# Strassen's seven products in the output projection of a hybrid decoder step, with weight loads on ACT's queue

## The chip, the cores and the metric

The kernel runs on one core of a Trainium2 chip. The metric is the device time of one launch in microseconds (us). Three runs of the kernel before took 2503.86, 2506.80 and 2510.32 us, the median is 2506.8.

## What is computed

One decoder layer runs over a prompt of 1024 tokens (16 learned meta tokens ahead of it) and over 8 sample sequences of 8 tokens each. The input is normed and projected into queries, keys, values and gates; 16 heads of width 128 (6 mLSTM "A", 6 gated-delta "B", 4 HGRN "C") run their recurrences; their outputs are normed, gated and projected back. In the reference, cut to what matters here:

```python
h = _rmsnorm(x, norm_w)
proj = jnp.einsum('bld,de->ble', h, w_in)                 # d = 2048, e = 8984
...
hcat = jnp.concatenate([ha, hb, hc], axis=2)              # 16 heads x 128
hcat = hcat * lax.rsqrt(jnp.mean(hcat * hcat, axis=-1, keepdims=True) + EPS)
y = hcat.reshape(bsz, L, MIX) * out_norm_w * jax.nn.silu(z)
out = jnp.einsum('ble,ed->bld', y, w_out)                 # the output projection, 2048 x 2048
return x + out
...
y_prompt = _rmsnorm(xp[:, N_META:], final_norm_w)
y_sample = _rmsnorm(xs, final_norm_w)
```

All is float32. The kernel gets that accuracy on TensorE from the faster fp32r format by splitting each operand in a high and a low part: a product is hi x hi + hi x lo + lo x hi, three matmuls.

## The kernel before

**Halves.** The prompt is worked off in two halves of 512 tokens; the first takes the 64 sample and 16 meta tokens along. For each half the input projection runs over 17 groups of columns (one head's q, k, v and gates after the other, in the order of `ORDER`: C0 B0 A0 B1 A1 C1 B2 A2, then B3 A3 C2 B4 A4 B5 A5 C3). The recurrence of a head (`mlstm_scan`, `gdn_scan`, `hgrn_scan`), its finish (`finish`, line 836) and the preparation of the second half's input (`prep_B`) are generators. `Weave.pump` steps them between the projection's matmuls by a clock of estimated costs, in four queues ("scan", "fin", "post", "bg"), one generator of a queue at a time. The build then orders each engine's queue, so the order in the code is near to, but not always, the order on an engine.

**Weights.** A piece is 128 x 512 numbers of `w_in` or `w_out`, 256 KB. `w_raw` and `o_raw` load it into one of four raw buffers (`wraw`). `feed_split` lets ScalarE (ACT) cast it to `whi` and VectorE (DVE) subtract to `wlo`, four buffers each. `feed_ahead` splits up to three pieces ahead of TensorE (PE) and asks for the raw data four pieces further on. All loads and stores of the kernel are issued by SyncE (SP), in one queue and in order: a load of a raw buffer waits until DVE has read the old piece, and what stands behind it waits too. Each DMA also waits until the one eight DMAs earlier has landed; these waits show as DMAHW0 to DMAHW7 below.

**Finish.** `finish` norms a head's output, turns it through DRAM (`turn_out`, `turn_in`), multiplies by the gate, splits it (cast on ACT, subtraction on GpSimd, POOL) and writes both parts to `y_dram`.

**Output projection.** After the last column group, for each half and each unit of `OUT_UNITS` (a column group of 512 and its token tiles), 16 heads `k` are summed in PSUM banks `oacc`: three matmuls of 128x128 by 128x512 for each prompt tile, two for the sample tile, whose high and low parts share one matmul's rows. Then DVE adds the input `x`, ACT sums squares, POOL multiplies by the final norm's weight, and `final_norm` scales and stores. The second half's `y` is loaded during the last column group of the first half.

Of the kernel before, what the change touches and what calls it, by code (L numbers as in the profile page):

```python
# [6 lines left out]
F32 = mybir.dt.float32  # L7
# [6 lines left out]
P = 128  # L14
# [172 lines left out]
OUT_UNITS = ([(cg, range(5)) for cg in range(4)], [(cg, range(4)) for cg in range(3)] + [(3, range(2)), (3, range(2, 4))])  # L187
# [3 lines left out]
def hybrid_step(ctx, tc, i, o):  # L191
# [3 lines left out]
    DMA = nc.sync.dma_start  # L195
    weave = Weave(ck)
# [33 lines left out]
    def w_raw(col, g):  # L230
        raw = wp.tile([P, 512], F32, tag="wraw", name="wraw")
        v = raw.rearrange("p (k c) -> p k c", c=P)
        if col is None:
            V.memset(raw, 0.0)
            for src, at in ((C_AI, 0), (C_BB, 32), (C_AF, 64), (C_BA, 96)):
                DMA(v[:, :, at:at + HA], i["w_in"][0, 512 * g:512 * (g + 1), src:src + HA].rearrange("(k p) c -> p k c", p=P))
        else:
            DMA(v, i["w_in"][0, 512 * g:512 * (g + 1), col:col + P].rearrange("(k p) c -> p k c", p=P))
        return raw

    def o_raw(k, cg):
        raw = wp.tile([P, 512], F32, tag="wraw", name="wraw")
        DMA(raw, i["w_out"][0, P * k:P * (k + 1), 512 * cg:512 * (cg + 1)])
        return raw

# [95 lines left out]
    for units in OUT_UNITS:  # L341
        for cg, _ in units:
            for k in range(NK):
                pieces.append((o_raw, k, cg))
# [256 lines left out]
    y_dram = [dp.tile([NH, P, w], F32R, name=f"y{w}") for w in (2 * NSAMP + 2 * HALF, 2 * HALF)]  # L601
# [233 lines left out]

    def finish(half, head, outs, ssq, scale, zs):
        r = sp.tile([P, 16], F32, tag="hr", name="hr")
        for g in half.groups:
# [16 lines left out]
        turn_in(hrs[-1], d)  # L855
        ck.last = ck.t["T"] + 5.0
# [12 lines left out]
        S.copy(yhi[:, 0:W], y[:, 0:W])  # L869
        yield  # L870
        G.tensor_tensor(ylo[:, 0:W], y[:, 0:W], yhi[:, 0:W], op=ALU.subtract)
        yield
        d = y_dram[half.index][head].bitcast(F32)
        for part, t in enumerate((yhi, ylo)):
            t = t.bitcast(F32)
            at_ = 2 * NSAMP if half.first else 0
            DMA(d[:, at_ + HALF * part:at_ + HALF * (part + 1)], t[:, 0:HALF])
            if half.first:
                DMA(d[:, NSAMP * part:NSAMP * (part + 1)], t[:, HALF:WS])
# [90 lines left out]
    def mlstm_scan(half, h, kT, qT, vT, tho, zs, nm, em, st):  # L970
# [118 lines left out]
        weave.add("fin", finish(half, h, hxs, ssq, 0.25, zs))  # L1089
# [60 lines left out]
    def gdn_scan(half, h, ck_, cq, cv, zs, Gb, eG, bb, st):  # L1150
# [242 lines left out]
        weave.add("fin", finish(half, HA + h, hxs, ssq, 1.0, zs))  # L1393
# [22 lines left out]
    def hgrn_scan(half, h, kT, lf, qT, vT, zs, st):  # L1416
# [152 lines left out]
        weave.add("fin", finish(half, HA + HB + h, hxs, ssq, 0.25, zs))  # L1569
# [91 lines left out]
    def load_y(half, g):  # L1661
        w = y_dram[half.index].shape[-1]
        yT[half.index][g] = [hp.tile([P, 2, w], F32R, tag=f"h{g}{part}", name=f"y{g}{part}") for part in (0, 1)]
        for q in range(4):
            DMA(yT[half.index][g][q // 2][:, q % 2].bitcast(F32), y_dram[half.index][4 * g + q].bitcast(F32))

    def y_block(half, k, n, part):

        at_ = HALF * part + P * n
        return yT[half.index][k // 4][k % 4 // 2][:, k % 2, at_:at_ + P]  # L1670

    hB, yT = {}, [{}, {}]
    for half, groups in zip(halves, group_lists):
        if not half.first:
            weave.drain_queue("bg")
            hT = hB
        seen = set()
        for n, group in enumerate(groups):
# [8 lines left out]
            if n == len(groups) - 1:  # L1687
# [3 lines left out]
                else:  # L1691
                    after = lambda g: load_y(halves[0], g)
# [12 lines left out]

    ys_flat = o["y_sample"].rearrange("b t d -> (b t) d")
    tags = ["a", "b", "c", "d", "e", "f", "g", "h", "j", "a", "b", "c", "d", "e", "f", "g", "h", "j", "k", "u"]

    def final_norm(toks, some, res, ss, fr, late):
        for n in some:  # L1710
            cnt = toks[n][1]
            V.tensor_reduce(fr[:cnt, n:n + 1], ss[:cnt, n], op=ALU.add, axis=AX.X)
            V.tensor_scalar(fr[:cnt, 8 + n:9 + n], fr[:cnt, n:n + 1], 1.0 / D, EPS, op0=ALU.mult, op1=ALU.add)
            G.tensor_tensor(fr[:cnt, 16 + n:17 + n], fr[:cnt, 8 + n:9 + n], halfneg[:cnt, 0:1], op=ALU.pow)
        yield
        for n in some:
            _, cnt, _, dst = toks[n]
            for cg in range(4):
                t, r = res[n, cg], fr[:cnt, 16 + n:17 + n]
                if cg == 3 and late:  # L1720
                    V.scalar_tensor_tensor(t[:cnt], t[:cnt], r, fnw[cg][:cnt], op0=ALU.mult, op1=ALU.mult)
                elif cg == 3 or late and cg == 2:
# [4 lines left out]
                yield  # L1727

# [12 lines left out]
    fnw = []  # L1741
    for half in halves:
        toks = []
        for n, (c0, cnt) in enumerate(half.tiles):
            if half.first and n == 0:
                toks.append((0, NSAMP, xs_flat, ys_flat))
            else:
                a = HALF * half.index + c0
                toks.append((c0, P, i["x_prompt"][0, a:a + P], o["y_prompt"][0, a:a + P]))
        nt = len(toks)  # L1750
        ss = sp.tile([P, 8, 4], F32, tag="oss", name="oss")
        fr = sp.tile([P, 24], F32, tag="fr", name="fr")
        res = {}
        for cg, some in OUT_UNITS[half.index]:
            ccols = slice(512 * cg, 512 * (cg + 1))
# [78 lines left out]
```

## Time and profile before

| | before |
|---|---|
| median of three runs | 2506.8 us (2503.86 to 2510.32) |
| the profiled execution | 2506.0 us, span 2504.3 us |
| first and last start of an output projection matmul | 2102.3 and 2493.5 us |
| output projection matmuls (`oacc`) | 1088 with `whi`, 576 with `wlo` |
| mean granted TensorE clock | 0.99 |
| DMA: moved, mean rate | 350.82 MB, 140 GB/s |
| HBM read, written | 285.71 MB, 62.19 MB |

The span runs from the first instruction to the end of the last on any engine; the time of an execution has a little more around it. PE is matmul, PEld the load of the stationary operand, DVE VectorE, ACT ScalarE, POOL GpSimd, SPq SyncE's queue. In rows by group: line, engine, operation, out<-in, shapes, count | busy us, mean ns of one | idle time before them and what ended it. In rows of waits: who waited, for whom, us in total, times, the longest. Most instructions go through one wrapper and carry its line, 137, so tile names tell them apart.

### The profile page before, as it was taken

Reading aid. Unit: us, or ns where it says so; the run is one execution under the profiler, and the core shown is the slowest. Engines: PE = TensorE matmul, PEld = TensorE weight load, DVE = VectorE, ACT = ScalarE, POOL = GpSimd, SP = SyncE. Lnnn points to the kernel's source line nnn. Section 1 sums busy time; section 2 is a strip of 40 time slices with the busy share of each in tenths; the row PEclk is TensorE's granted clock in tenths of the full one; section 3 lists DMA queues with packets and bytes.
Section 4 is the critical chain, followed back from the end, with each engine's and each line's share of the span. In section 5 each row is a group of like instructions: output and inputs, shape, how many; then the busy total and the mean of one; then the engine's idle time right before and its main releaser. Section 6 shows DMA issues by size and latency. Waiting matters only on the chain.

```text
span 2504.3 us, 43941 instructions
## 1 busy us (share of the span) xinstructions
PE 2442.1 (98%) x16032; PEld 2184.5 (87%) x16032; DVE 1425.5 (57%) x3080; ACT 991.2 (40%) x2430; POOL 554.8 (22%) x743
## 2 busy tenths in 40 slices
PE   6999999999999999999999999999999999999998
PEld 5898999999999999999787888888888888888886
DVE  7775655765656655556864556554654545323435
ACT  5643434443435333333642434333443334222324
POOL 5331212420313312113320113110320102211201
PEclk9999999999999999999999999999999999999999
DMA  5656665655645454447554455454554558636735
GB/s 129 152 140 147 147 146 133 162 131 130 158 99 138 99 131 118 118 119 203 132 132 115 120 123 136 122 130 101 138 127 114 129 123 257 183 84 200 254 97 185
DMA packets 681045, 350.82 MB, mean 140 GB/s; under 512 B 260004, under 2 KB 622076, under 8 KB 680828
## 3 DMA queue, kind: packets, MB, share of 16 engines
q1 hardware_dynamic: 680828, 348.01, 54.3%
q8 instruction: 126, 2.06, 0.4%
q14 instruction: 91, 0.75, 0.1%
HBM read 285.71 MB, written 62.19 MB: 139 GB/s over the span
## 4 chain that ended last, share of the span: by engine, by line
PE 80%; issue 5%; DVE 5%; DMA 4%; ACT 2%; POOL 2%; SPq 1%; POOLq 0%; DVEq 0%; ACTq 0%
PE acc L137 59%; PE oacc L137 9%; PE pa L137 1%; DVE wlo L137 1%; PE po L137 1%; PE nd L137 1%; PE pz L137 1%; PE pyy L137 1%; DMA wraw<-in_w_in_dram 1%; POOL res L137 1%; PE pu L137 1%; DMA px<-in_x_prompt_dram 1%; ACT whi L137 1%; PE poh L137 1%; PE pw L137 1%
## 5 line engine op out<-in xcount | busy, mean ns | idle before, releaser
L137 DVE TENSOR_TENSOR wlo<-wraw,whi 128x512 fp32r<-128x512 f32 x720 | 525.6, 734 | 569.6 <-ACT whi L137 552.1
L137 PE MATMUL acc<-hA,whi 128*128 128x288 f32 (+1 forms) x4544 | 826.2, 304 | 11.3 <-ACT whi L137 6.4
L137 ACT CAST whi<-wraw 128x512 fp32r<-128x512 f32 x720 | 441.9, 618 | 929.1 <-PE acc L137 641.2
L137 PE MATMUL acc<-hB,whi 128*128 128x512 f32 x2272 | 722.2, 400 | 4.3 <-ACT whi L137 2.1
L137 PEld LDWEIGHTS acc<-hA,whi 128*128 128x128 f32 x4544 | 679.6, 191 | 18.2 <-ACT whi L137 8.1
L137 PE MATMUL acc<-hA,wlo 128*128 128x288 f32 x2240 | 489.7, 299 | 1.6 <-DVE wlo L137 1.6
L137 PEld LDWEIGHTS acc<-hB,whi 128*128 128x128 f32 x2272 | 413.6, 189 | 86.2 <-ACT whi L137 2.7
L137 PE MATMUL acc<-hB,wlo 128*128 128x512 f32 x1120 | 441.1, 394 | 2.6 <-DVE wlo L137 2.6
L137 PEld LDWEIGHTS acc<-hA,wlo 128*128 128x128 f32 x2240 | 367.7, 190 | 2.7 <-DVE wlo L137 2.6
L137 PE MATMUL oacc<-whi,y 128*128 128x512 f32 x1088 | 343.4, 390 | 1.1 <-ACT whi L137 1.1
L137 PEld LDWEIGHTS acc<-hB,wlo 128*128 128x128 f32 x1120 | 211.0, 188 | 52.0 <-DVE wlo L137 6.8
L137 PEld LDWEIGHTS oacc<-whi,y 128*128 128x128 f32 x1088 | 204.2, 188 | 44.5 <-ACT whi L137 2.4
L137 PE MATMUL oacc<-wlo,y 128*128 128x512 f32 x576 | 224.8, 390 | 1.2 <-DVE wlo L137 1.2
L137 PEld LDWEIGHTS oacc<-wlo,y 128*128 128x128 f32 x576 | 108.1, 188 | 25.2 <-DVE wlo L137 3.1
L137 POOL TENSOR_TENSOR res<-res,fnw 128x512 f32<-128x512 f32 (+1 forms) x34 | 54.3, 1627 | 255.4 <-ACT oscr L137 255.4
L137 POOL TENSOR_TENSOR y<-y,zs 128x592 fp32r<-128x592 f32 (+1 forms) x32 | 46.0, 1437 | 171.4 <-ACT zs L137 106.7
L137 POOL TENSOR_TENSOR qd<-qT,emb 128x512 f32<-128x512 f32 x12 | 17.7, 1479 | 230.3 <-PE po L137 230.3
L137 DVE TENSOR_TENSOR Yt<-Yc,Bb 128x60 f32<-128x60 f32 (+8 forms) x180 | 37.6, 209 | 43.9 <-DMA Bb<-db 39.0
L137 POOL TENSOR_TENSOR hr<-hr,halfneg 128x4 f32<-128x4 f32 (+1 forms) x48 | 44.1, 919 | 61.1 <-DVE hr L137 58.4
L137 POOL TENSOR_TENSOR nrm<-nrm,halfneg 128x10 f32<-128x10 f32 x12 | 23.5, 1960 | 138.9 <-DVE nrm L137 138.9
L137 POOL TENSOR_TENSOR X<-Ex,hk 128x256 f32<-128x256 f32 (+1 forms) x40 | 39.1, 978 | 63.2 <-PE pa L137 41.8
L137 ACT ACTIVATE Wt<-pw,nrm 128x128 f32<-128x128 f32 (+1 forms) x54 | 19.8, 367 | 78.1 <-PE pw L137 78.1
(416 smaller groups left out, 2766.7 us busy)
## 6 DMA issues: line engine op xcount, KB each, us to landing
wraw<-in_w_in_dram SPq DMA_DIRECT2D x564, 256.0 KB
wraw<-in_w_out_dram SPq DMA_DIRECT2D x144, 256.0 KB
y<-y SPq DMA_DIRECT2D x16, 576.0 KB
px<-in_x_prompt_dram SPq DMA_DIRECT2D x32, 256.0 KB
yd<-y SPq DMA_DIRECT2D x128, 64.0 KB
out_dram<-sst SPq DMA_DIRECT2D x16, 512.0 KB
s<-yd SPq DMA_DIRECT2D x32, 256.0 KB
y<-zs SPq DMA_DIRECT2D x32, 256.0 KB
```

What stands on the lines that cost most here:

```text
L137: return f(out, *a, **k)
```

## The change

**Strassen.** Write the prompt's product as a 2 x 2 block matrix: rows of tokens (first and second half), heads in `ORDER`'s first eight (K1) and last eight (K2), columns in two halves of 1024. Seven products of half size take the place of eight, by the Winograd form. The first and second use plain blocks of `y` and of `w_out`; the others use sums S1 to S4 of `y` blocks and T1 to T4 of `w_out` blocks. `phase(u, j, ...)` is one product's unit: 512 columns, four tiles, eight heads; `LAST_UNITS` cuts the last product's second unit in two. The samples' matmuls stand in the first three products (`own`, with the product's own weights, and `other`, with a weight piece of their own).

**The sums.** `combine_weights` makes T1 to T4 in the second half as a "bg" generator: 16 rounds of four loads, four POOL subtractions and four stores to DRAM. `finish` of the second half makes S1 to S4 and A22: the first half's plain `y` comes back from DRAM (`y_whole`), POOL adds and subtracts, and each result is split by a cast and a DVE subtraction and stored (`y_comb`). `load_y` with a name first drains the finishes that it needs. S2 is loaded in three steps during the second product, its last tile at the start of the third.

**Weights.** Pieces of full columns and all output pieces are issued by ACT (`WDMA`), into five raw buffers. The gate's small pieces stay on SP.

```diff
+K1, K2 = HEADS[:NH // 2], HEADS[NH // 2:]
+LAST_UNITS = [(0, range(4)), (1, range(2)), (1, range(2, 4))]
...
+    WDMA = nc.scalar.dma_start
...
-        raw = wp.tile([P, 512], F32, tag="wraw", name="wraw")
+        raw = wp.tile([P, 512], F32, tag="wraw", name="wraw", bufs=5)
...
-            DMA(v, i["w_in"][0, 512 * g:512 * (g + 1), col:col + P].rearrange("(k p) c -> p k c", p=P))
+            WDMA(v, i["w_in"][0, 512 * g:512 * (g + 1), col:col + P].rearrange("(k p) c -> p k c", p=P))
...
+    def c_raw(name, j, kk):
+        raw = wp.tile([P, 512], F32, tag="wraw", name="wraw", bufs=5)
+        WDMA(raw, w_comb[name][NK // 2 * j + kk])
+        return raw
...
     def finish(half, head, outs, ssq, scale, zs):
...
+        def parts(src, hi, name):
+            S.copy(hi, src)
+            ck.sync()
+            V.tensor_tensor(src.bitcast(F32R), src, hi, op=ALU.subtract)
+            d = y_comb[name][kk].bitcast(F32)
+            ck.last = max(ck.last, ck.t["T"]) + 3.0
+            yield
+            DMA(d[:, 0:HALF], hi.bitcast(F32))
+            DMA(d[:, HALF:], src)
+        if upper:
+            G.tensor_tensor(ya, ya, y, op=ALU.subtract)
...
+            yield from parts(ya, yhi, "S3")
+            return
+        G.tensor_tensor(yb, yb, y, op=ALU.add)
+        yield
+        yield from parts(y, yhi, "A22")
+        G.tensor_tensor(ya, yb, ya, op=ALU.subtract)
+        yield
+        yield from parts(yb, spare, "S1")
+        G.tensor_tensor(yc, yc, ya, op=ALU.subtract)
+        yield
+        yield from parts(ya, yhi, "S2")
+        yield
+        yield from parts(yc, spare, "S4")
...
+    def load_y(u, n, src):
+        if isinstance(src, str):
+            weave.drain(*(fins[1, h] for kk in (2 * n, 2 * n + 1) for h in (K1[kk], K2[kk])))
...
+    def combine_weights():
...
+                for dst, a, b in ((b11, b12, b11), (b12, b22, b12), (b22, b22, b11), (b21, b21, b22)):
+                    ck.last = ck.t["T"] + 7.0
+                    yield
+                    G.tensor_tensor(dst, a, b, op=ALU.subtract)
...
+    each = every(0, "S2", [x_rows((5, 10), 1, 0)], (6, 9, 12))
+    for j in range(2):
+        accs, sacc, sacc2 = banks(), bank("oacc"), bank("oacc")
+        phase(1, j, accs, halfn, own=(sacc, lambda kk: yT[1][kk // 2][:, kk % 2, 0:2 * NSAMP]), other=(sacc2, ys_block(K1)), each=each)
...
+    each = every(1, "S1", [lambda step: load_y(0, 3, "S2") if step == 0 else None])
+    for j in range(2):
+        accs, sacc = banks(), bank("oacc")
+        phase(0, j, accs, halfn, other=(sacc, ys_block(K2)), each=each)
```

What the order of the engines shows. First ACT's queue, in the output projection: before, between the sums of squares (`oscr`) after the first unit.

```order
L137 ACTIVATE oscr_24474,oss_23948<-res_24471 64x512 [waits DVE_49]
L137 CAST whi_24510<-wraw_24332 128x512 [waits DMAHW0_49,PE_49]
L137 ACTIVATE oscr_24488,oss_23948<-res_24485 128x512 [waits DVE_49]
L137 ACTIVATE oscr_24494,oss_23948<-res_24491 128x512 [waits DVE_49,Activation_49]
L137 ACTIVATE oscr_24500,oss_23948<-res_24497 128x512 [waits DVE_49,Activation_49]
L137 COPY no_24519<-pnp_24516 6x128 [waits PE_49]
L137 COPY no2_24522<-pnp_24516 48x128
L137 CAST whi_24539<-wraw_24369 128x512 [waits DMAHW3_49,PE_49]
```

Now the second product, with the last head's splits (`zs`, `yc`) between.

```order
L247 DMA wraw_25026<-in_w_out_dram 128x512 [waits DMAHW3_49,DVE_49]
L137 CAST whi_25022<-wraw_24844 128x512 [waits DMAHW4_49,PE_49]
L137 CAST whi_25031<-wraw_24892 128x512 [waits DMAHW7_49,PE_49]
L247 DMA wraw_25035<-in_w_out_dram 128x512 [waits DMAHW7_49,DVE_49]
L247 DMA wraw_25055<-in_w_out_dram 128x512 [waits DMAHW1_49,DVE_49]
L137 CAST whi_25051<-wraw_24921 128x512 [waits DMAHW5_49,PE_49]
L137 CAST whi_25060<-wraw_24994 128x512 [waits DMAHW0_49,PE_49]
L137 CAST zs_24406<-y_24905 128x512 [waits DVE_49]
L137 CAST yc_24882<-yb_24881 128x512 [waits Pool_49]
```

A load stands between the casts, and waits for DVE (the raw buffer) and for one of the eight DMA semaphores, which SP's DMAs use as well.

Then SP's queue at the end of the last scan, head C3 (`state_C3` is its final state, `yd64` the turn of its output, `s6` what comes back, `res` rows of `x`, `out_3` and `out_9` small outputs). Before:

```order
L1786 DMA res_25208<-in_x_prompt_dram 128x512 [waits DMAHW1_49,PE_49]
L1571 DMA out_7_dram<-state_C3_761 128x128 [waits DMAHW2_49,Pool_49]
L243 DMA wraw_24369<-in_w_out_dram 128x512 [waits DMAHW3_49,DVE_49]
L1786 DMA res_25220<-in_x_prompt_dram 128x512 [waits DMAHW4_49,PE_49]
L1786 DMA res_25595<-in_x_prompt_dram 128x512 [waits DMAHW5_49,PE_49]
L1786 DMA res_24857<-in_x_prompt_dram 128x512 [waits DMAHW6_49]
L243 DMA wraw_24409<-in_w_out_dram 128x512 [waits DMAHW7_49,DVE_49]
L810 DMA yd64_24432<-y_24430 32x16x32 [waits DMAHW0_49,DVE_49]
```

And now (`y02`, `y03` are the third and fourth tile of S2, each two loads):

```order
L1863 DMA res_24953<-in_x_prompt_dram 128x512 [waits DMAHW3_49,DVE_49]
L1751 DMA y02_25428<-S2_87 128x1024 [waits DMAHW4_49,PE_49]
L840 DMA yd64_24907<-y_24905 32x16x32 [waits DMAHW6_49,DVE_49]
L840 DMA yd64_24907<-y_24905 32x16x32 [waits DMAHW7_49]
L840 DMA yd64_24907<-y_24905 32x16x32 [waits DMAHW1_49]
L840 DMA yd64_24907<-y_24905 32x16x32 [waits DMAHW2_49]
L1854 DMA out_3_dram<-no_25003 6x128 [waits DMAHW4_49,Activation_49]
L1857 DMA out_9_dram<-no2_25006 48x128 [waits DMAHW5_49,Activation_49]
L1751 DMA y02_25428<-S2_87 128x1024 [waits DMAHW6_49]
L844 DMA s6_24903<-yd64_24907 128x4x128 [waits DMAHW2_49,DMAHW7_49,DMAHW1_49,DMAHW0_49]
L1751 DMA y03_25579<-S2_87 128x1024 [waits PE_49]
```

The weights are gone from SP, and the turn of the last head has the third tile of S2 ahead of it.

Last PE. Before, one head `k` in a unit of the first half: two sample matmuls, then three for each of four tiles (two of the tiles shown).

```order
L137 MATMUL oacc_24503<-whi_24579,y11_23765 128x512
L137 MATMUL oacc_24503<-wlo_24580,y11_23765 128x512
L137 MATMUL oacc_24504<-whi_24579,y11_23765 128x512
L137 MATMUL oacc_24504<-wlo_24580,y11_23765 128x512
L137 MATMUL oacc_24504<-whi_24579,y11_23765 128x512
L137 MATMUL oacc_24505<-whi_24579,y11_23765 128x512
L137 MATMUL oacc_24505<-wlo_24580,y11_23765 128x512
L137 MATMUL oacc_24505<-whi_24579,y11_23765 128x512
```

Now the end of one head and the start of the next in the second product: the fourth tile, the samples of K2 with the same piece, the samples of K1 (`ys`) with a piece of their own, the next piece.

```order
L137 MATMUL oacc_24984<-whi_24917,y10_24267 128x512
L137 MATMUL oacc_24984<-wlo_24918,y10_24267 128x512
L137 MATMUL oacc_24984<-whi_24917,y10_24267 128x512
L137 MATMUL oacc_24985<-whi_24917,y10_24267 128x512
L137 MATMUL oacc_24985<-wlo_24918,y10_24267 128x512
L137 MATMUL oacc_24986<-whi_24990,ys_24935 128x512
L137 MATMUL oacc_24986<-wlo_24991,ys_24935 128x512
L137 MATMUL oacc_24981<-whi_25022,y11_24270 128x512
```

A head takes 16 matmuls and two pieces here, where it took 14 and one.

More of the change, by code (lines that the diff above doesn't have):

```diff
@@ L855, in finish @@
         turn_in(hrs[-1], d)
+        if not half.first:
+            DMA(ya, y_whole[0][K1[kk]])
+            if not upper:
+                DMA(yb, y_whole[1][kk])
+                DMA(yc, y_whole[0][head])
         ck.last = ck.t["T"] + 5.0
```

367 lines of the change are left out of this document (269 added, 98 removed).

## The prediction

> **What bounds the kernel now.** I read the first page of the profile, then busy time by stage, then the output projection's matmuls alone, and last what TensorE (PE) waited for.
>
> ```profile
> span 2504.3 us, 43941 instructions
> ...
> PE 2442.1 (98%) x16032; PEld 2184.5 (87%) x16032; DVE 1425.5 (57%) x3080; ACT 991.2 (40%) x2430; POOL 554.8 (22%) x743
> ...
> PE 80%; issue 5%; DVE 5%; DMA 4%; ACT 2%; POOL 2%; SPq 1%; POOLq 0%; DVEq 0%; ACTq 0%
> ```
>
> PE is busy for 98% of the span, and 80% of the chain that ended last is PE. The other engines have room. By stage (columns: PE, weight loads, DVE, ACT, POOL in us, clock, DMA share, GB/s):
>
> ```profile
> 0.00:100.00 100.00, 76.90 (x474) 70.24 (x474) 73.80 (x157) 61.21 (x133) 40.52 (x121) 0.97 0.62 142
> 100.00:500.00 400.00, 387.59 (x3120) 379.66 (x3119) 265.62 (x600) 166.23 (x447) 111.60 (x153) 0.98 0.61 145
> ...
> 1500.00:2000.00 500.00, 499.58 (x2775) 414.35 (x2774) 286.38 (x587) 196.76 (x472) 98.29 (x109) 1.00 0.50 125
> ...
> 2100.00:2450.00 350.00, 349.26 (x1598) 289.31 (x1598) 134.68 (x214) 112.11 (x224) 68.46 (x54) 1.00 0.54 165
> 2450.00:2504.30 54.30, 42.28 (x180) 33.10 (x178) 30.11 (x52) 21.77 (x40) 9.59 (x9) 0.95 0.62 198
> ```
>
> The projection runs from 2102 to 2494, and PE is full there. "Busy" alone does not prove that, since matmuls overlap, so I count them. The next rows are the projection's accumulators (`oacc`) alone: first all of them, then a stretch that holds nothing else.
>
> ```profile
> L137 PE MATMUL oacc<-whi,y x1088: 387/389/529, 2102.3 to 2493.5; 128*128 128x512 f32 x182
> L137 PE MATMUL oacc<-wlo,y x576: 387/389/504, 2102.5 to 2493.3; 128*128 128x512 f32 x192
> ...
>   DVE wlo L137: 1.2, 5
>   ACT whi L137: 1.1, 3
> ```
> ```profile
> 2163.80:2313.00 149.20, 149.20 (x659) 123.51 (x659) 7.36 (x12) 1.17 (x2) 1.00 0.47 138
> ```
>
> One matmul takes 389 ns alone but leaves every 149.20/659 = 0.2264 us. In the whole projection PE waited 1.2 + 1.1 = 2.3 us. So here a matmul less is 0.2264 us less.
>
> The Trainium skill ("Perfetto Trace Analysis", Identifying the Most-Contended Engine) warns that matmul busy share is a poor measure and wants the busy share of weight loads: here 123.51/149.20 = 83%. By that measure PE would have 17% room, and a matmul would be worth 123.51/659 = 0.187 us, the first term below 36.0 us and the time 2473.5. The constant 0.2264 us speaks for the larger figure.
>
> **1. Matmuls.** A prompt product of before is 8 token tiles x 4 column groups x 16 heads x 3 = 1536 matmuls. Strassen has 7 products of 4 tiles x 2 column groups x 8 heads x 3 = 192 each, 1344. The samples keep theirs: 4 x 16 x 2 = 128, spread over the first three products. So 1664 becomes 1472, and 192 x 0.2264 = **43.5 us** go. Bounds: these matmuls stand on the path in a stage with 2.3 us of waits, so at most 43.5.
>
> **2. Weight issue moves from SP to ACT.**
>
> ```profile
> L238 SPq DMA_DIRECT2D wraw<-in_w_in_dram x564: 367/384/1805, 18.2 to 2084.1; - x188
> L243 SPq DMA_DIRECT2D wraw<-in_w_out_dram x144: 327/328/866, 2084.6 to 2486.0; - x144
> ```
> ```profile
> L137 ACT CAST whi<-wraw 128x512 fp32r<-128x512 f32 x720 | 441.9, 618 | 929.1 <-PE acc L137 641.2 <-PE oacc L137 194.8 <-DMA wraw<-in_w_out_dram 27.9
> ```
>
> ACT gets 564 x 0.384 + 152 x 0.328 = 266 us of issuing. No row shows ACT issuing a DMA, so the ends are 0 (all of it in the 929.1 us that ACT already idles before casts, 1.29 us for each of 720) and 266 (none of it hidden). The idle time is 3.5 times the need, so I take a value near the low end, **+5 us**. Queued behind a weight load on ACT stand the next `whi` cast and the evacuations of the recurrent scans, and PE behind those; the casts run three pieces ahead of PE, the evacuations do not, so the cost falls there. The cover is thin only where two weight pieces serve 16 (14) matmuls: 16 x 0.2264/2 = 1.81 us a piece, of which cast and issue take 0.618 + 0.328 = 0.95.
>
> **3. The fifth buffer and a freed SP.**
>
> ```profile
> SPq L238 <- DVE wlo L137: 543.3, 251, 7.7
> SPq L243 <- DVE wlo L137: 242.7, 122, 9.4
> ```
> ```profile
> PE pt L137 <- DVE x L137: 12.6, 8, 7.2
> PE acc L137 <- ACT whi L137: 8.5, 9, 1.9
> PE pz L137 <- DVE Yc L137: 7.6, 3, 5.2
> PE acc L137 <- DVE whi L137: 4.8, 2, 3.9
> PE acc L137 <- DVE wlo L137: 4.2, 8, 1.1
> ```
>
> SP waited 786 us in 373 waits, 2.1 us each, for the raw buffer that DVE's `wlo` frees, and every other transfer queued behind. With five buffers the load waits for the subtraction one piece earlier, 12 x 0.2264 = 2.7 us or so, more than the mean wait: most of it goes, and what is left would now stand on ACT. PE gains only where it waited for weights: 8.5 + 4.8 + 4.2 = 17.5 us. Bounds 0 and -17.5; I take **-4 us**, since the same transfers still share the DMA engines and the 12.6 us for `x` at the start stay.
>
> The Trainium skill ("DMA: Bandwidth & Descriptors", Issuing engines are not separate DMA queues) says that issuing from a second engine saves only sequencer time, as all run on the same DMA engines. By it this term is 0 and the time 2470.0.
>
> **4. Combined weights.** 64 POOL subtractions and 128 DMAs of 256 KB early in the second half.
>
> ```profile
> L137 POOL TENSOR_TENSOR res<-res,fnw 128x512 f32<-128x512 f32 x30 | 46.4, 1568 | 255.4 <-ACT oscr L137 255.4
> ```
>
> 64 x 1.568 = 100 us on a POOL that is busy 98.29 of 500 us, and 33.6 MB over some 900 us, 37 GB/s on top of 125. Both lie beside PE: **0 us**. If the cover fails, a scan operation on POOL meets one of them in about a fifth of cases and waits half of it: 64 x 0.2 x 0.78 = 10 us, the upper bound. There is no gain in it.
>
> **5. The longer finish.** A head of the second half now costs POOL 1 or 3 subtractions and additions where there was 1, and one or four cast-subtract pairs instead of a cast. Only the last head (C3) can be late. First a row of ACT's timeline, the evacuation of its last matmul, then the first store of its result in SP's.
>
> ```profile
> 2154.76 0.59 ACT L137 COPY s<-poh 128x512 f32<-128x512 f32 x1 [2.32 <-PE poh L137]
> ```
> ```profile
> 2172.57 0.33 SPq L877 DMA_DIRECT2D y<-zs  x1
> ```
>
> From its last matmul to its first store went 17.8 us. Three POOL operations (4.7) and two pairs of 0.618 + 0.69 (2.6) come on top, then a store and a load: about 35 us as an estimate. PE first needs the result in the third product's eighth head: 39 matmuls of the first product, 256 of the second and 98 of the third later, 393 x 0.2264 = 89 us. The `S2` tile that now stands ahead of its turn on SP waits for buffers that PE read last in the first product, so it should not hold it. **0 us**, with 50 to spare; beyond that each us late is a us lost.
>
> **6. Boundaries.** 15 units (7 x 2 + 1) instead of 9 end with additions out of PSUM.
>
> ```profile
> L137 DVE TENSOR_TENSOR wlo<-wraw,whi x720: 625/691/1799, 30.5 to 2491.6; 128x512 fp32r<-128x512 f32 x180
> ```
>
> By the 2.3 us of 9 units, 15 cost 3.8, so +1.5; the first three products use five or six banks a unit instead of four and start the next on banks not yet free, another +1: **+2.5 us**. Bounds: 0, and 15 x 2 additions of 0.69 us = 21. The second and third product (480 matmuls, 109 us) also move the most: 64 pieces of 256 KB, 16 `S` loads of 512 KB, `x` rows, the samples' tiles and the last head's stores, about 30 MB or 275 GB/s. Nearby rates have been seen on either side with PE nearly full:
>
> ```profile
> 2300.00:2350.00 50.00, 49.61 (x218) 40.54 (x217) 21.84 (x48) 17.36 (x34) 12.93 (x10) 1.00 0.76 249
> ```
> ```profile
> 2102.00:2112.00 10.00, 10.00 (x45) 8.10 (x44) 8.05 (x12) 8.17 (x14) 4.36 (x6) 1.00 0.96 337
> ```
>
> The last two units are the same in kind as before, so the 10.4 us after the last matmul (2493.5 + 0.4 to 2504.3) stay.
>
> **Sum.** -43.5 + 5 - 4 + 0 + 0 + 2.5 = -40.0. The profiled execution took 2506.0 us (span 2504.3 and 1.7 around it), so **2466.0 us**; the median of the three runs, 2506.8, lies 0.8 higher.
>
> **Rivals.**
>
> *ACT's queue gives back half* (chance 0.18, 2478 to 2498). If a tenth of the 266 us of issuing lands on PE through late evacuations, 26.6 stands for 5: 2487.6. For it: every weight load now sits between operations of the scans. The order also shows each load waiting on one of eight DMA semaphores that SP's transfers share, so a late SP transfer can hold ACT. Against: 929.1 us of idle time.
>
> *ACT is held by DVE* (0.08, slower: 2514 and more). The waits of part 3 do not go but move: a load waits for a late `wlo`, and the casts and evacuations behind it wait too. The place is ACT's queue in the scans; the price is a share of 786 us. It decides from (40.0 + 5 + 7.5)/716 = 0.07 us a load; at a tenth of 786 us in place of the 5 the time is 2466.0 - 5 + 78.6 = 2539.6. Against it: DVE is busy 57%, and a buffer more covers the mean wait.
>
> *The second and third product become transfer-bound* (0.06, no change). Their 30 MB take 151 us at the 198 GB/s of the last row by stage, 42 more than PE's 109: 2508. Against: 249 and 337 GB/s with PE full.
>
> *More is freed* (0.10, 2440 to 2455). The 17.5 us go altogether and ACT costs nothing: 2466.0 - 13.5 - 5 - 2.5 = 2445.0.
>
> That the products are not fewer is excluded by the count.
>
> **How the numbers follow.** The forecast (2455 to 2478) has 0.58. Measurement tells about 0.3%, 7.5 us, from no change. Faster: 0.58 + 0.18 + 0.10 = 0.86; same 0.06; slower 0.08. For 8 in 10 the range takes the forecast, the nearer three quarters of the ACT rival (to 2494) and the upper part of the last (from 2448).
>
> **What would show it.** Right: 1472 `oacc` matmuls at 0.226 us; PE's waits inside the projection under 6 us; ACT near 1260 us with its issuing counted, most of it before casts; SP's waits for `wlo` gone; the third product without a wait for `S2`. Wrong: PE waiting for scan evacuations by ACT from 100 to 2000 us, ACT waiting for `wlo` or for SP's transfers, `whi` waiting for `wraw` in the second and third product, or a matmul interval that rises.

## The result and the profile after

The changed kernel took 2609.5 us (median of four runs, 2605.31 to 2616.66) against 2505.5 us for the kernel before on the same chip: 1.0419 times as long, 95% interval 1.0403 to 1.0435. 2466 was forecast, so the sign is wrong, and the range (2448 to 2494) ends 115 us below the measurement. In one later run, e8, a single execution of 13391.5 us stands far from the other eight and is left out.

The first page of the profile after, its span, busy times and the shares of the chain that ended last:

```profile
span 2614.5 us, 44206 instructions
...
PE 2446.3 (94%) x15840; PEld 2184.1 (84%) x15840; DVE 1536.1 (59%) x3160; ACT 1017.7 (39%) x2474; POOL 707.7 (27%) x855
...
PE 49%; DMA 7%; DVE 5%; issue 5%; POOL 3%; ACT 2%; SPq 1%; ACTq 0%; DVEq 0%; POOLq 0%
```

There are 192 matmuls fewer, as counted, but PE is only 49% of the chain, where it was 80%, and POOL has gained 153 us. The busy times by stretch of the kernel after (PE, weight loads, DVE, ACT, POOL, clock, DMA share, GB/s; the third is the projection) show two things at once:

```profile
500.00:800.00 300.00, 251.71 (x2000) 243.55 (x1998) 166.11 (x353) 89.88 (x267) 131.29 (x139) 0.90 0.73 207
...
1500.00:2000.00 500.00, 475.40 (x2702) 393.69 (x2701) 282.99 (x604) 190.75 (x454) 103.21 (x110) 0.98 0.53 137
2226.00:2603.00 377.00, 355.89 (x1573) 290.15 (x1572) 209.71 (x299) 141.34 (x278) 122.84 (x96) 0.97 0.71 228
```

Before, the first stretch was:

```profile
500.00:800.00 300.00, 297.37 (x2474) 291.18 (x2473) 175.54 (x443) 122.67 (x346) 60.06 (x91) 0.98 0.54 127
```

PE has lost 46 us of work there, POOL has more than doubled, and the granted clock has fallen to 0.90. Most of the loss lies ahead of the projection, as the starts of the same matmuls tell (us; n counts the input projection's matmuls; e2, e5 and e19 are explained below):

| start of | before | after | e2, no combined weights | e5, short finishes | e19, best |
|---|---|---|---|---|---|
| n = 3000 | 547 | 549 | 552 | 552 | 550 |
| n = 5000 | 879 | 942 | 884 | 936 | 876 |
| n = 9000 | 1790 | 1882 | 1824 | 1857 | 1806 |
| n = 9500 | 1922 | 2042 | 1984 | 1995 | 1942 |
| first `oacc` | 2102.3 | 2226.0 | 2168.0 | 2173.2 | 2121.9 |
| last `oacc` | 2493.5 | 2603.3 | 2542.2 | 2536.2 | 2478.8 |

Before the projection 123.7 us are lost: some 60 between 550 and 880 us, 28 around 2000, the rest in small pieces. Inside it 13.9 us are gained (391.2 to 377.3), not 43.5.

**The first place.** Waits of POOL between 500 and 800 us, after (who waited, for whom, us, times, longest):

```profile
POOL px L137 <- DMA px<-in_w_out_dram: 47.7, 10, 12.2
POOL px L137 <- DMA pxs<-in_w_out_dram: 29.5, 5, 10.4
```

These are `combine_weights`' subtractions. They are written at the start of the second half, whose first matmul runs at 1235 us, and the build's ordering has put them some 450 us earlier, in one burst (532 to 782 us). POOL's timeline shows what they do to the scan (start, duration, operation, wait ahead of it):

```profile
734.64 1.26 POOL L137 TENSOR_TENSOR px<-px 128x512 f32<-128x512 f32 x1 [5.04 <-DMA pxs<-in_w_out_dram]
735.98 1.26 POOL L137 TENSOR_TENSOR px<-pxs,px 128x512 f32<-128x512 f32 x1
737.32 1.26 POOL L137 TENSOR_TENSOR pxs<-pxs,px 128x512 f32<-128x512 f32 x1
738.65 1.26 POOL L137 TENSOR_TENSOR px<-px,pxs 128x512 f32<-128x512 f32 x1
739.87 1.95 POOL L137 TENSOR_TENSOR nrm<-nrm,halfneg 128x10 f32<-128x10 f32 x1
```

`nrm`, the norms of a B head's keys, stands behind a subtraction that waits 5.0 us for its load, and behind the four. DVE waits for it, and works in order: `Ball` of the same head and the next `wlo` stand behind its own `nrm`, and PE waits 10.4 us for `Ball`, up to 745 us:

```profile
DVE nrm L137 <- POOL nrm L137: 17.3, 2, 10.2
DVE Yt L137 <- DMA Bb<-db: 16.5, 2, 13.6
```
```profile
PE pkq L137 <- DVE Ball L137: 10.4, 1, 10.4
```

In the kernel before, in the same stretch:

```profile
DVE Yt L137 <- DMA Bb<-db: 4.7, 2, 3.1
...
DVE nrm L137 <- POOL nrm L137: 4.1, 2, 2.1
```

PE's waits between 500 and 800 us add up to 48.2 us after, and to 2.6 before.

**The second place.** PE around its longest wait, after (`pkk`, `pqk`, `pvb`, `pz` are one B head's scan):

```profile
1974.62 0.40 PE L137 MATMUL acc<-hB,wlo 128*128 128x512 f32 x1
1974.85 1.06 PE L137 MATMUL pkk<-Ck 128*128 128x128 f32 x8
1975.74 1.06 PE L137 MATMUL pqk<-Cq,Ck 128*128 128x128 f32 x8
1976.64 0.60 PE L137 MATMUL pvb<-ident,Cv 128*128 128x128 f32 x4
1996.45 1.35 PE L137 MATMUL pz<-X,Ball 32*32 32x32 f32 x32 [19.21 <-DVE X L137]
```

The same head before:

```profile
1885.19 1.06 PE L137 MATMUL pqk<-Cq,Ck 128*128 128x128 f32 x8
1886.00 0.71 PE L137 MATMUL acc<-hB,whi 128*128 128x512 f32 x2
1886.55 0.39 PE L137 MATMUL acc<-hB,wlo 128*128 128x512 f32 x1
1886.78 0.62 PE L137 MATMUL acc<-hB,whi 128*128 128x512 f32 x2
1887.23 0.39 PE L137 MATMUL acc<-hB,wlo 128*128 128x512 f32 x1
1887.46 0.60 PE L137 MATMUL pvb<-ident,Cv 128*128 128x128 f32 x4
1887.81 0.70 PE L137 MATMUL acc<-hB,whi 128*128 128x512 f32 x2
```

The chain from `pvb` to `pz` is hardly longer than it was (19.8 us from start to start, before 18.2). But before, 78 projection matmuls stood between the two in PE's order, and after there is none: nothing is there to run meanwhile.

**The third place.** PE's waits in the projection after, where the sum before was 2.3 us:

```profile
PE oacc L137 <- DVE wlo L137: 13.7, 6, 5.6
PE puh L137 <- ACT s L137: 3.4, 1, 3.4
PE oacc L137 <- ACT whi L137: 3.0, 4, 1.6
PE oacc L137 <- ACT t L137: 1.0, 1, 1.0
```

### The profile page after: what moved, and what is told of

It reads as the page before. It is cut to its first block, busy times and chain, and to the rows that moved or that the text cites. A ratio compares the mean times of both kernels' runs of the same rounds, so it can differ in the third digit from the quotient of the medians.

```text
span 2614.5 us, 44206 instructions
## 1 busy us (share of the span) xinstructions
PE 2446.3 (94%) x15840; PEld 2184.1 (84%) x15840; DVE 1536.1 (59%) x3160; ACT 1017.7 (39%) x2474; POOL 707.7 (27%) x855
## 4 chain that ended last, share of the span: by engine, by line
PE 49%; DMA 7%; DVE 5%; issue 5%; POOL 3%; ACT 2%; SPq 1%; ACTq 0%; DVEq 0%; POOLq 0%
PE acc L137 36%; PE oacc L137 5%; POOL res L137 2%; DVE wlo L137 2%; DMA wraw<-in_w_in_dram 1%; PE pa L137 1%; DMA Bb<-db 1%; DMA wraw<-in_w_out_dram 1%; PE pyy L137 1%; SPq L1289 1%; PE pz L137 1%; DVE Yt L137 1%; PE po L137 1%; DVE Yc L137 1%; ACT whi L137 1%
## 5 line engine op out<-in xcount | busy, mean ns | idle before, releaser
L137 DVE TENSOR_TENSOR wlo<-wraw,whi 128x512 fp32r<-128x512 f32 x728 | 558.7, 771 | 505.8 <-ACT whi L137 477.1
L137 PE MATMUL acc<-hB,whi 128*128 128x512 f32 x2272 | 733.8, 405 | 2.7 <-DMA hB<-hblo 2.3
L137 PEld LDWEIGHTS acc<-hB,whi 128*128 128x128 f32 x2272 | 421.6, 192 | 86.7 <-DMA hB<-hblo 2.6
L137 PEld LDWEIGHTS acc<-hA,wlo 128*128 128x128 f32 x2240 | 370.8, 192 | 13.7 <-DVE wlo L137 13.7
L137 PE MATMUL oacc<-whi,y 128*128 128x512 f32 x928 | 300.5, 398 | 4.0 <-ACT whi L137 3.0
L137 PEld LDWEIGHTS acc<-hB,wlo 128*128 128x128 f32 x1120 | 214.2, 191 | 51.8 <-DVE wlo L137 5.4
L137 PEld LDWEIGHTS oacc<-whi,y 128*128 128x128 f32 x928 | 177.8, 192 | 43.9 <-ACT whi L137 4.7
L137 PE MATMUL oacc<-wlo,y 128*128 128x512 f32 x480 | 191.5, 399 | 13.7 <-DVE wlo L137 13.7
L137 PEld LDWEIGHTS oacc<-wlo,y 128*128 128x128 f32 x480 | 92.2, 192 | 35.4 <-DVE wlo L137 16.1
L137 PE MATMUL pz<-X,Ball 32*32 32x32 f32 x576 | 21.1, 211 | 59.8 <-DVE X L137 41.1
L137 PEld LDWEIGHTS pz<-X,Ball 32*32 32x32 f32 x576 | 18.4, 123 | 67.4 <-issue 37.6
L137 POOL TENSOR_TENSOR res<-res,fnw 128x512 f32<-128x512 f32 (+1 forms) x30 | 41.0, 1379 | 71.9 <-ACT oscr L137 71.9
```

The lines of the kernel that those rows point to most:

```text
L137: return f(out, *a, **k)
```

## The experiments

All times are medians; the ratio to the kernel before has its 95% interval behind it. The changed kernel is 2609.5 (1.0419). The runs were spread over several chips, each with the kernel before beside it (medians 2503.0 to 2507.1 us). The difference of two runs can come out up to 5 us apart by the medians and by the ratios, so its single microseconds mean little.

### Whose queue, and which part

**e1**, weights on SP again.

```diff
-    WDMA = nc.scalar.dma_start
+    WDMA = nc.sync.dma_start
```

> The changed kernel with its weight transfers issued on SP again (five raw buffers, combined weights, long finishes and seven products stay). If ACT's queue is the loss (ACT issues 716 transfers, and waits for DVE's wlo 120.6 us and for raw tiles 36.5 us in the trace of after): about 2500 us, and the stretch from 550 to 860 us gets back most of its 61 us. If the burst of the combined weights is the loss: no gain, 2600 us or above, since the weights then stand behind the T stores in SP's queue: ACT's and PE's waits for wraw between 500 and 780 us grow from what they are. Between these (2560) if the two share it.

Measured: 2618.3 us (1.0432, 1.0406 to 1.0457). No gain from moving the issue back, so ACT's queue does not explain the loss.

**e2**, without combined weights (`weave.add("bg", combine_weights())` removed, `c_raw` reads `w_out`).

> The changed kernel without the combined weights: their 64 loads, 64 subtractions and 64 stores are left out, and the projection's 72 combined pieces are plain rows of w_out, so that 5 of the 7 products are of other numbers. If the burst of the combined weights at 503 to 782 us is the loss: 60 to 75 us faster than the changed kernel, 2535 to 2550 us, with the input projection's matmuls at 860 us back within 10 us of the kernel before. If ACT's queue is the loss: within 10 us of the changed kernel, 2600 to 2610 us.

Measured: 2555.7 us (1.0190, 1.0175 to 1.0205), 54 us less, near the first theory. At n = 5000 the kernel is 5 us behind the kernel before instead of 63. The 19 us at the B head stay.

**e4**, the same work at its written place.

```diff
+                for t in (b11, b12, b22, b21):
+                    G.tensor_copy(t[0:1, 0:1], splits[at[0] - 1][1][0:1, 0:1].bitcast(F32))
                 for t, heads, cg in ((b11, K1, j), ...
```

> The changed kernel with each of the 16 rounds of combined weights held back to its place in the program by four one-element POOL copies from the weight piece in use there, so that the rounds lie in the second half, one about every 44 us. If it is the burst and its place that cost: about 2545 us, as if the combined weights were left out. If it is the work itself (33.6 MB, 128 transfers on SP, 64 POOL operations) wherever it lies: 2590 to 2615 us, and the loss moves behind 1235 us.

Measured: 2602.8 us (1.0382, 1.0367 to 1.0398). The loss moved (n = 5000 on time, 41 us more behind than e2 at n = 9000) but did not go. The place alone does not explain it. It is not cleared either, since the copies that hold each round back hold POOL as well: POOL waited 52.7 us for the copies' weight pieces, beside 75.9 us for the loads.

**e5**, short finishes: `ya`, `yb`, `yc`, their sums, loads and stores removed. The store of the first half's `y_whole` goes with them, and the step that was added for it to each finish of the first half.

> The changed kernel with short finishes in the second half: the sums and differences of the heads' outputs (S1, S2, S4 and the subtraction of S3), their loads and their stores are left out, and the projection reads the head's own output in their place. If the longer finishes delay the scan (28 us between 1882 and 2042 us, among it the 19.2 us in which PE waits for X): 2575 to 2585 us, with the stretch from 1882 to 2042 us within 8 us of the kernel before. If not: within 8 us of the changed kernel's 2609.5 us.

Measured: 2554.6 us (1.0195, 1.0175 to 1.0216), 55 us less, more than expected; the wait of 19 us is gone and 14 us of it came in the projection.

**e8**, both left out.

> The changed kernel without the combined weights and with the short finishes at once (both left out as in the runs with one of them; the projection multiplies other numbers). If the two losses add up (-54 and -55 us): 2500 us, about 7 us faster than the kernel before, and ACT's queue and the projection's own waits hold the other 36 us of the 43.5 that the matmuls save. If they share a cause, and one alone still brings it: 2530 to 2550 us.

Measured: 2499.5 us (0.9978, 0.9959 to 0.9998). The two add up (54 + 55, together 110), and make up all of the slowdown and a little more.

**e3**, parts 2 and 3 of the change on the kernel before.

```diff
-            DMA(v, i["w_in"][0, 512 * g:512 * (g + 1), col:col + P].rearrange("(k p) c -> p k c", p=P))
+            WDMA(v, i["w_in"][0, 512 * g:512 * (g + 1), col:col + P].rearrange("(k p) c -> p k c", p=P))
```

> The kernel before with two parts of the change alone, the weights' transfers on ACT's queue and the fifth raw buffer. The prediction put +5 and -4 us on them: 2507 us, within 0.3% of the kernel before. Theory that ACT's queue holds the casts (whi waits 120.6 us for wlo in the trace of after): 2515 to 2530 us. Theory that it frees SP's queue and gains: under 2500 us.

Measured: 2505.2 us (1.0008, 0.9997 to 1.0019), no clear difference, as the prediction's two terms say. ACT does wait for DVE's `wlo` in its queue (e3's waits of ACT), but the kernel is not slower for it:

```profile
ACT whi L137 <- DVE wlo L137: 88.1, 63, 4.0
```

### What in the combined weights

**e6** and **e7** split e4: only the transfers, and only the subtractions (on four tiles loaded once).

> The combined weights held back into the second half, with their 64 loads and 64 stores but without the 64 POOL subtractions, which are left out (the combined pieces are then plain rows of w_out). Theory that POOL's two-input operations cost, since DVE's operations beside them take longer (wlo 996 ns beside POOL, 691 without, in the trace of after): as without combined weights, 2555 to 2565 us. Theory that the transfers cost (33.6 MB, SP's queue in order, the eight shared DMA semaphores): as with them, 2590 to 2605 us.

Measured: 2563.3 us (1.0232, 1.0203 to 1.0260), 8 above e2; the interval touches e2's, so this cost is hardly clear of noise.

> The combined weights held back into the second half, with the 64 POOL subtractions on four tiles that are loaded once, without the other 60 loads and the 64 stores, which are left out (the projection reads plain rows of w_out in their place). Theory that POOL's operations slow DVE: 2590 to 2605 us. Theory that the transfers cost: 2555 to 2565 us. If each has half, both this and the run with the transfers alone lie near 2580 us.

Measured: 2573.2 us (1.0267, 1.0242 to 1.0292), 18 above e2. Neither theory holds alone: 8 and 18 against 47 for both in e4. Only with both does POOL wait for loads (75.9 us in e4) and do SP's stores wait for POOL (94.2 us). Both runs keep e4's copies, which POOL waited 42.7 us for in e6 and 53.9 in e7, so 8 and 18 hold the cost of the copies too. A wait of POOL need not be a loss, then: e6 has 42.7 us of them and loses 8.

**e9**, the subtractions of the weights and the finishes' sums on DVE (`G.tensor_tensor` to `V.tensor_tensor`; they are 64 and 32, the expectation miscounts the second).

> The changed kernel with the 64 subtractions of the combined weights and the 40 sums and differences of the long finishes on DVE instead of POOL; everything is computed. Theory that POOL's two-input operations cost by slowing DVE: DVE takes on 104 operations of 0.69 us (72 us, at 59% busy), and DVE's other operations get their time back: 2550 to 2590 us. Theory that the transfers and the queues cost: no better than the changed kernel, 2605 to 2650 us.

Measured: 2583.2 us (1.0315, 1.0298 to 1.0333), 26 less, though DVE is the busier engine. So 26 us hang on POOL doing these operations; 79 us above the kernel before stay.

### The order

The planner's clock explains the second place. At most two heads are in work. Before a new one begins, `start_head` writes out what is left of the older one's scan and finish (line 1669). While it does so the planner's PE clock jumps forward over due times with no projection matmul written. Added up over the head starts of the second half, the jumps of that clock (the planner's estimate, no measurement) are 34 us before, 116 after and 27 in e10; 25 us of each lie at the first of these starts. The new part of a long finish has up to nine steps, four of them due 3 us late.

**e10**, the parts in one step.

```diff
-            ck.last = max(ck.last, ck.t["T"]) + 3.0
-            yield
...
-        yield
-        yield from parts(y, yhi, "A22")
+        parts(y, yhi, "A22")
```

> The changed kernel, everything computed, with the parts of a long finish written in one step of its stream instead of in up to nine steps with 3 us between them. Theory that the long finishes cost by the order (the head's start drains them, the planner's clock jumps, and the scan's steps are written without projection matmuls between them; in the changed kernel none stand between the B head's pvb and pz at 1996 us, 78 in the kernel before): 2550 to 2565 us, with 60 to 80 matmuls there again and no wait of 19 us. Theory that the work of the parts costs (POOL, DVE, ACT and 144 transfers): 2595 to 2610 us.

Measured: 2577.3 us (1.0294, 1.0280 to 1.0308), 32 less, between the two theories. 75 matmuls stand between `pvb` and `pz` again and the 19 us are gone. That is 32 of the finishes' 55 us; the other 23 this step does not reach. It leaves the first half's finishes as they are (see e19).

**e13**, the same without combined weights.

> The same, without the combined weights (loads, subtractions and stores left out; the projection reads plain rows of w_out in their place). Theory of the order: 2495 to 2510 us, as with short finishes and no combined weights (2501). Theory of the work: 2535 to 2555 us, as without combined weights alone (2556).

Measured: 2521.6 us (1.0068, 1.0054 to 1.0081), 34 less than e2, between the two theories.

**e11**, e10 with e4's place and `nc.gpsimd.dma_start` for the weights' 128 transfers.

> The one-step finishes, everything computed, with the combined weights held back into the second half and their 128 transfers issued on POOL's own queue, behind POOL's subtractions, so that SP's queue no longer waits for POOL. Theory that the combined weights cost above all because SP's stores wait for POOL and hold what is queued behind them (transfers alone +8 us, subtractions alone +18 us, both +47 us): 2515 to 2530 us. Theory that it is the load on DMA and DVE: 2545 to 2560 us. A slow issue on POOL would show as more POOL time.

Measured: 2575.5 us (1.0287, 1.0273 to 1.0301), no gain, and neither theory's time. It does not settle SP's share: the one-element copies waited 77.4 us on POOL, POOL still waited 49.0 us for loads, and each of these transfers took POOL 0.56 to 0.58 us to issue.

### Off POOL, step by step

**e14**, e10 with the weights in the second half and each round's first subtraction 18 us of the planner's clock behind its loads.

```diff
+                    V.tensor_copy(t[0:1, 0:1], lo)
                     DMA(t, i["w_out"][0, ...
+                ck.last = ck.t["T"] + 18.0
+                yield
+                lo = splits[at[0] - 1][1][0:1, 0:1].bitcast(F32)
+                V.scalar_tensor_tensor(b12[0:1, 0:1], lo, 0.0, b12[0:1, 0:1], op0=ALU.mult, op1=ALU.add)
```

> The one-step finishes, everything computed, with the combined weights in the second half and each round's first subtraction held back by some 18 us behind its loads (four one-element copies and one one-element operation on DVE, from the weight piece in use), so that no POOL subtraction waits for a load. Theory that the combined weights cost because waiting subtractions hold POOL's queue and with it the scan's own POOL steps: 2535 to 2550 us (2521.6 without combined weights, +8 us for the transfers, +10 to +18 us for the 64 operations themselves). Theory that the work itself costs, waiting or not: 2565 to 2580 us, as 2577.3 with waiting subtractions in the first half.

Measured: 2557.2 us (1.0230, 1.0188 to 1.0272), 20 less than e10 by the medians, 16 by the ratios, between the two theories. Place and waiting changed together here. POOL still waited 39.5 us, now for the holding operation. The weights still cost 36 us over e13.

**e15** and **e16**: the projection's sums and `fnw` products on DVE, with and without combined weights.

```diff
-            G.tensor_tensor(t[:cnt], t[:cnt], fnw[cg][:cnt], op=ALU.mult)
+            V.tensor_tensor(t[:cnt], t[:cnt], fnw[cg][:cnt], op=ALU.mult)
```

> The same, with the projection's sums with t1, q and the residual rows and its products with fnw on DVE instead of POOL (128 operations). Theory that the boundaries of the products cost because ACT's squares and DVE's final scaling wait for POOL there (ACT waits for POOL's res 1.8 to 2.7 us four times and DVE for POOL's fr 3.1 us before the 5.6 us in which PE waits at 2516 us in the trace of after): 10 to 20 us faster than the run with POOL, with under 12 us of waits in the projection instead of some 20. Theory that DVE has no room there: the same or slower.

Measured: 2545.5 us (1.0173, 1.0146 to 1.0200), 12 less. The interval overlaps e14's, but in the traces the projection itself shrinks from 373.1 to 355.5 us, and e16 below is clear of e13. PE's two leading waits in e15's projection, and its length, 355.5 us:

```profile
PE oacc L137 <- ACT t L137: 2.4, 2, 1.4
PE oacc L137 <- DVE wlo L137: 2.2, 3, 1.2
```
```profile
L137 PE MATMUL oacc<-whi,y x928: 387/389/793, 2175.5 to 2531.0; 128*128 128x512 f32 x186
```

Of 43.5 us 35.7 are there. The kind of wait that went, in the timeline of after: DVE's and ACT's scaling stands behind POOL's `fr`, and the next cast and `wlo` behind them.

```profile
2516.54 1.60 POOL L137 TENSOR_TENSOR fr<-fr,halfneg 128x1 f32<-128x1 f32 x3
2517.13 1.34 ACT L137 ACTIVATE res<-res,fr 128x512 f32<-128x512 f32 x2 [1.73 <-POOL fr L137]
2517.13 1.32 DVE L137 TENSOR_SCALAR res<-res,fr 128x512 f32<-128x512 f32 x3 [3.11 <-POOL fr L137]
...
2518.37 0.60 ACT L137 CAST whi<-wraw 128x512 fp32r<-128x512 f32 x1
...
2519.84 1.68 DVE L137 TENSOR_TENSOR wlo<-wraw,whi 128x512 fp32r<-128x512 f32 x1
```

> The one-step finishes without combined weights (left out; the projection reads plain rows of w_out in their place), with the projection's sums and products on DVE instead of POOL. Theory of POOL at the boundaries: 2502 to 2512 us, 10 to 20 us under the 2521.6 us with POOL. Theory that DVE has no room: 2520 us or more.

Measured: 2507.5 us (1.0009, 0.9995 to 1.0024), 14 less than e13.

**e17**, e15 with the weights' subtractions on DVE; **e18**, the finishes' sums too.

> The last full version (2545.5 us) with the 64 subtractions of the combined weights on DVE as well, still 18 us behind their loads. Theory that the 64 operations cost by POOL (its queue held, DVE slowed beside it; 2545.5 against 2507.5 without combined weights): 2515 to 2530 us, the transfers' 8 us left. Theory that DVE's room is used up: 2545 us or more.

Measured: 2518.0 us (1.0055, 1.0033 to 1.0077), 27 less.

> The same with the 40 sums and differences of the finishes on DVE too, so that none of the change's additions is on POOL; everything is computed. Theory of POOL: another 5 to 15 us, 2505 to 2520 us, level with the kernel before or a little above. Theory that DVE's room is used up: the same or slower than the run without this step.

Measured: 2507.6 us (1.0000, 0.9989 to 1.0012), another 10 (32 sums, not 40). Everything is computed, and it is level with the kernel before.

**e19**, e18 with the first half's finishes in the steps they had before.

```diff
             S.copy(yhi[:, 0:W], y[:, 0:W])
-            ck.last += 1.0
             yield
             DMA(y_whole[0][head], y[:, 0:HALF])
-            ck.last = ck.t["T"] + 2.0
-            yield
```

> The last full version (2507.6 us) with the first half's finishes written as in the kernel before, with the store of the whole output in the same step as the subtraction, so that the planner's clock jumps at the heads' starts as it did there. Theory of the order: the 10 us that the input projection is behind the kernel before at 1000 us go (in the kernel before with ACT's queue and the fifth buffer alone they are not there): 2494 to 2502 us, under the kernel before. If those 10 us come from ACT's queue with the extra transfers: no change, 2505 to 2510 us.

Measured: 2490.8 us (0.9950, 0.9936 to 0.9965), 17 less by the medians, 12.5 by the ratios (e18 ran on another chip), and faster than both kernels. In the traces the second half begins 11.5 us earlier than in e18 and the projection 12.9. The planner's jumps at the head starts of the first half fall from 33 to 20 us, as in the kernel before. Its page and two of its stretches, the second the projection:

```profile
span 2489.8 us, 44259 instructions
...
PE 2406.5 (97%) x15840; PEld 2150.6 (86%) x15840; DVE 1571.9 (63%) x3402; ACT 1025.6 (41%) x2478; POOL 487.3 (20%) x693
```
```profile
500.00:800.00 300.00, 300.00 (x2524) 293.94 (x2524) 176.80 (x442) 123.35 (x347) 63.09 (x95) 1.00 0.50 124
...
2122.00:2479.00 357.00, 347.86 (x1575) 285.67 (x1573) 220.08 (x372) 147.19 (x283) 21.81 (x24) 1.00 0.73 242
```

From after to e19: one-step finishes -32, weights later and not waiting -20, the projection's sums off POOL -12, the weights' subtractions off POOL -27, the finishes' sums off POOL -10, the first half's steps -17; together 119 us (medians, unrounded). e19 ends 25 us above the forecast of 2466: it enters the projection 19.6 us later than the kernel before and gains 34.3 us in it.

## Why the prediction was wrong

**Part 4 failed: "Both lie beside PE: 0 us", upper bound 10.** Measured 54 us (e2), of which the transfers alone make about 8 (e6, with the holding copies). Two errors. The text put the subtractions "early in the second half"; the order of the engines already has POOL's `px` operations ahead of the first half's last finishes, and the order was not read at that place. What that error cost is open: at the written place the subtractions cost nearly the same (e4), but behind copies that hold POOL too; in the second half and without waits for loads they cost 16 to 20 us less (e14 against e10). The second: POOL's 20% of busy time was read as room, and the bound took an operation met half-way, 0.78 us. But POOL works in order and does parts of the scan's chains, so what stands behind a subtraction waits for that subtraction's load as well (5.0 us at 734 us), and DVE's operations beside POOL's get longer (last section). Put on DVE, at 63% busy, the subtractions cost 27 us less than on POOL (e17). How much was POOL's queue, how much SP's stores that wait for POOL and how much DVE's slowing isn't separated.

**Part 5 failed: "0 us", "only the last head (C3) can be late".** Measured 55 us (e5): 32 by the order (e10), 10 by POOL's sums (e18); the other 13 were not split further. Part of them lies in the first half, where e5 leaves out a step as well: without long finishes the second half begins 9 us earlier (e8 against e13, neither with combined weights). The working followed the last head to the third product and overlooked that every head's start drains the finish of the older head. The same rule fits the 12 to 17 us that e19 gains, where a step and a later due time had been added to each finish of the first half.

**Part 6 was right in its kind and mis-sized:** +2.5 was taken, bounds 0 and 21. The third place has 13.7 + 3.0 + 1.0 = 17.7 us of `oacc` waits, and the clock falls with them; 12 to 14 us went when the sums left POOL (e15, e16). e5 gains 14 us in the projection too, so the finishes' share and this one overlap. I had priced DVE's additions out of PSUM, not ACT's squares and the scaling that stand behind POOL.

**Part 1 was right.** The interval is unchanged (median 0.227 us in every run), and where little else waits most of the gain comes: 35.7 us in e15. The weight-load share that the Trainium skill ("Perfetto Trace Analysis", Identifying the Most-Contended Engine) prefers would have allowed 36.0. e18 (2488.7 - 2134.8 = 353.9 us, 37.3 gained) lies a little above that with 6.1 us of PE waits left, where the kernel before had 2.3. So the interval is the nearer of the two once these waits are counted.

**Parts 2 and 3 were right together:** +5 - 4 forecast, +2 us by e3's ratio, with an interval of -1 to +5. Only their sum was measured. SP's waits for `wlo` are gone, as said. The rule that issuing from a second engine saves only sequencer time ("DMA: Bandwidth & Descriptors" in the Trainium skill, Issuing engines are not separate DMA queues) agrees with it.

**The rival** that was to end slower, "ACT is held by DVE", named the wrong engine. ACT waits 120.6 us for `wlo` in the kernel after, but with the weights back on SP (e1) nothing is gained. POOL was in no rival. The signs that part 2 named did come: ACT's 1017.7 us and 716 issues of 0.33 to 0.37 us make some 1280, and the third product has no wait for S2; none of them could have shown the loss.

## What to carry to other kernels

An engine with little busy time is not free if it runs in order and stands in somebody's chain: list what it does for others, and price new work on it by the wait that comes with it, its loads' latency included. Where a planner with a clock writes the order, look at what a new step does to that clock, and count the independent matmuls between a chain's steps before and after; that is known before a run. A saving in a full stage is real, but it shows only when the additions that pay for it hold back none of the chains that this stage waits for; here they did less harm on the busier engine.

## What the runs showed of the hardware

**DVE slows beside POOL.** In the trace of after, `wlo` has a median of 691 ns in 531 operations without a POOL operation beside them and 996 ns in 88 that lie at least 80% beside POOL operations longer than 0.6 us; ACT's cast stays at 620 and 618 ns. The 88 are of two kinds: in 19 DVE's operation started first, and none was slowed (median 692 ns); in the other 69 POOL's did, and 48 of these took over 900 ns. Two engines' rows of one moment, DVE first, then POOL:

```profile
1968.24 1.19 DVE L137 TENSOR_TENSOR wlo<-wraw,whi 128x512 fp32r<-128x512 f32 x1
1969.35 1.78 DVE L137 TENSOR_TENSOR yb<-yb,yc 128x512 fp32r<-128x512 f32 x1
...
1971.39 0.68 DVE L137 TENSOR_TENSOR wlo<-wraw,whi 128x512 fp32r<-128x512 f32 x1
```
```profile
1967.07 1.80 POOL L137 TENSOR_TENSOR ya<-yb,ya 128x512 f32<-128x512 f32 x1
1968.95 1.63 POOL L137 TENSOR_TENSOR yc<-yc,ya 128x512 f32<-128x512 f32 x1
```

The Trainium skill states it ("SBUF — State Buffer", SBUF: two separate sides): DVE and GpSimd hold a shared pair of ports in turn, each for a whole instruction, and a DVE operation with two SBUF inputs takes part against a GpSimd operation that reads SBUF. The rows and the count by who started first agree; the prediction should have used it.

**The clock falls after PE's waits.** In the trace of after, PE waits 10.4 us up to 745 us; from 745 to 751 us the granted clock is 0.50 and four projection matmuls take 1.16 us, from 751 to 760 us it is 0.99 and they take 0.70. Over the whole kernel PE's waits grew by 105 us (51.8 to 157.3, added from the trace), and matmul intervals above their median cost some 43 us more than before, in stretches such as 500 to 800 us with a granted clock of 0.90 against 0.98. So on average a wait cost about 1.4 times its length here.
